# Two-layer hybrid block: attention stacks on the hardware DMA queue, out-projection operands prepared inside the attention, and four smaller moves

## The chip, the cores and the metric

One core of a Trainium2 chip runs the whole program. The metric is the device time of one execution in microseconds; the runs shown of a kernel are summed up by their median.

## The reference, cut to what matters

```python
def block(h_lat, h_ctx, l):                   # 1024 latent and 256 context tokens, D = 1024, two layers
    u = modulate(rms_norm(h), ...)            # modulation vectors from c and c_ctx
    p = u @ w_in                              # mLSTM | attention | pool | convolution, 256 wide each
    q, k = rope(rms_norm(q)), rope(rms_norm(k))          # 4 heads, 2 maps of width 32 each
    a = softmax(q0 @ k0.T) - lam * softmax(q1 @ k1.T)    # two maps per head
    y = concat(mlstm, subln(a @ v), pool, conv)
    h = h + gate1 * (y @ w_out)
    g, up = split(modulate(rms_norm(h), ...) @ ffn_w_in)
    h = h + gate2 * ((silu(g) * up) @ ffn_w_out)         # D_FF = 2816
...
```

In the second layer the context tokens are keys and values only; their queries, output projection and FFN are left out.

## The kernel before, in words

Every float32 matmul is three passes: operands are split into a high part (an ACT copy to float32r) and a low part (a subtraction on DVE or POOL, `sub_lo`, L292), and hi·hi, lo·hi and hi·lo are summed in PSUM. One helper, L165, records nearly all engine operations, so rows are told apart by tile names.

Each layer runs through five phases. **A** (`mixers`, L593): the projections of the normed input `uh`/`ul`, with the mLSTM, the convolution and the pool woven in; the weights come through `load_w` (two raw buffers, five of each part). `qk_in` (L945) norms and rotates queries and keys, splits them, and writes both parts to a DRAM scratch `qk_scr` (tile `qks`, L971 and L972) by DMAs issued on POOL, which use the software queue (q0). **B** (`attention`, L1152): `stacks(h)` reads for each of a head's two maps a stack of queries `Qs` (high part twice, then low part twice, 64 + 64 partitions, L1169 and L1170) and one of keys `Ks` (high and low part twice, 128 partitions, L1172), also on POOL, and the values `V` on SP (the hardware queue, q1). The doubling is in the source's access pattern: `dup` puts a leading dimension of size 2 and step 0 before the rows.

```python
            return AP(tensor=ap.tensor, offset=ap.offset, ap=[[0, 2]] + [list(x) for x in ap.ap])
```

The work is cut into units of a head and 256 queries, five per head in layer 0, four in layer 1. Each unit takes four slots of a hand-written plan, in which scores `sc`, softmax `pr`, transposes `aT`, values `po` and the head norm `subln` of several units overlap. The plan fixes the order on PE, ACT and DVE. `stacks(0)` is issued in slot 0, `stacks(1)` in slot 2, each later head's in slot 2 of the head before the one ahead of it; there are buffers for two heads. A score needs map 0 first and map 1 in the next slot.

**C** (`out_proj`, L1345): chunks of tokens, in layer 0 (256, 512), (768, 512), (0, 256) as (start, size), in layer 1 the first two. It loads `y` and splits it, loads the residual `h`, and for each of eight output tiles loads two weights (`wr`, two buffers), splits them (`wh` on ACT, `wl` on POOL) and multiplies. `norm_ffn` (L1395) norms the previous chunk beside the matmuls of the next, and makes the Strassen operands `Uh`/`Ul` of the FFN. **F** (`ffn_in`, L1464): 22 halves of products in Strassen form; in layer 0 the second layer's modulation (`mod_vec`, L441, two DVE passes over each `mw`) is advanced by 18 steps at the end of each half until it is done. **G** (`ffn_out`, L1580): the down-projection with `gr`, `xr` loaded and split as `gh`/`gl`, `xh`/`xl`; its pools open when `ffn_in`'s close.

Of the kernel before, what the change touches and what calls it, by code (L numbers as in the profile page):

```python
# [18 lines left out]
P = 128  # L19
# [165 lines left out]
class Builder:  # L185
# [32 lines left out]
    def stage(self, temps):  # L218

        if self.fx is not None:  # L220
            self.fx.close()
        self.fx = ExitStack()
        self.fp = self.mkpool(self.fx, "right")
        self.temps = (self.fp, 512, temps)
# [368 lines left out]
    def mixers(self, l, u, norm):  # L593
# [130 lines left out]
        return self.attention()  # L724
# [427 lines left out]
    def attention(self):  # L1152
# [3 lines left out]
        gd = nc.gpsimd.dma_start  # L1156
# [7 lines left out]
        def stacks(h):  # L1164
            Qs, Ks = [], []
            for m in range(2):
                mp = 2 * h + m
                Qm = self.U(f"Qs{m}", F32R)
                gd(Qm[0:64, q0:NT], dup(self.qk_scr[0, mp, 0, :, q0:NT]))  # L1169
                gd(Qm[64:P, q0:NT], dup(self.qk_scr[0, mp, 1, :, q0:NT]))  # L1170
                Km = self.U(f"Ks{m}", F32R)
                self.stack = gd(Km[:, 0:NT], dup(self.qk_scr[1, mp].rearrange("a r n -> (a r) n")))  # L1172
                Qs.append(Qm)
                Ks.append(Km)
            V = self.U("V")[:, :NCH * 64].rearrange("p (c x) -> p c x", x=64)
            nc.sync.dma_start(V, self.v_scr[h])
            heads[h] = (Qs, Ks, V)
# [166 lines left out]

    def out_proj(self, l, src, dst, chunks, later):  # L1345
# [3 lines left out]
        order = (0, 1, 4, 5, 6, 7, 2, 3)  # L1349
        todo = iter(())  # L1350
        first = ExitStack()
        ypool = self.mkpool(first, "left")
        for i, (c0, n) in enumerate(chunks):
            v = 1 if c0 < NCTX else 0
            cs = slice(c0, c0 + n)
            y = [None] * KT
            for k in order:
                if i == 0:
                    hi, lo = (ypool.tile([P, 512], F32R, name=f"{nm}{k}", tag=nm, bufs=KT) for nm in ("y0h", "y0l"))
                else:  # L1360
                    hi, lo = self.E("yh", KT, F32R), self.E("yl", KT, F32R)
                raw = self.E("yr", 3)
                hi, lo, raw = hi[:, :n], lo[:, :n], raw[:, :n]
                nc.sync.dma_start(raw, self.y_scr[k][:, cs])
                self.copy(hi, raw)
                self.sub_lo(lo, raw, hi)
                y[k] = (hi, lo)
            h = [self.E("h", 10) for _ in range(KT)]
            for k in range(KT):
                nc.sync.dma_start(h[k][:, :n], src(k)[:, cs])  # L1370
            for nt in range(KT):
                w = []
                for pc in range(2):
                    raw, hi, lo = self.E("wr", 2), self.E("wh", 3, F32R), self.E("wl", 3, F32R)
                    nc.sync.dma_start(raw, self.a["w_out"][l, nt, pc])
                    self.copy(hi, raw)
                    self.sub_lo(lo, raw, hi, nc.gpsimd)
                    w.append((hi, lo))
# [10 lines left out]
            if i == 0:  # L1389
                first.close()  # L1390
# [5 lines left out]
    def norm_ffn(self, l, need):  # L1396
# [9 lines left out]
        def chunk(h, c0, n):  # L1406
# [11 lines left out]
            cs = slice((c0 - NCTX) // 2, (c0 - NCTX) // 2 + HALF)  # L1418
            a, b = slice(0, HALF), slice(HALF, 2 * HALF)
            for k in range(4):  # L1420
                for x in (k, k + 4):
                    nc.vector.scalar_tensor_tensor(h[x], h[x], A[:, x, v:v + 1], r, ALU.mult, ALU.mult)
                    nc.scalar.activation(h[x], h[x], AF.Identity, bias=B(x))
                yield
                u1, u2 = h[k], h[k + 4]
                t, z = self.T("t12"), self.T("t34")
                g = nc.gpsimd.tensor_tensor
                g(t[:, a], u1[:, b], u1[:, a], ALU.subtract)
                nc.vector.tensor_tensor(z[:, a], u2[:, b], u1[:, b], ALU.subtract)
                g(t[:, b], u2[:, b], t[:, a], ALU.subtract)  # L1430
                g(z[:, b], u2[:, a], t[:, b], ALU.subtract)
                yield
                Uh, Ul = state["U"][k]
                two = lambda x: x.rearrange("p (i n) -> p i n", i=2)
                for i, j, src in ((0, 1, u1[:, a].unsqueeze(1)), (1, 3, two(u2)), (3, 5, two(t)), (5, 7, two(z))):
                    hi, lo = Uh[:, i:j, cs], Ul[:, i:j, cs]
# [27 lines left out]
    def ffn_in(self, l, state, mid, need, side):  # L1464
# [6 lines left out]
        more = 0 if need else 3  # L1471

        def weights(f, x):
            raw = {}
            for i, (ff, pc) in enumerate(((f, 0), (f, 1), (f + 1, 0), (f + 1, 1))):
                raw[i] = self.E("fr", 8 + more)
                nc.sync.dma_start(raw[i], self.a["ffn_in"][l, ff, x, pc])
            for i in (self.S1, self.S2, self.S3, self.S4):
                raw[i] = self.E("fr", 8 + more)
# [7 lines left out]
        def split(raw):  # L1487
            hi, lo = self.E("fh", 5 + more, F32R), self.E("fl", 5 + more, F32R)
# [65 lines left out]
        for f in range(0, NF, 2):  # L1554
            sg = sc = None
            for x in range(2):
# [11 lines left out]
                for _ in range(18):  # L1568
                    next(side, None)
            for i, (ff, ab) in enumerate(((f + 1, 1), (f + 1, 0), (f, 1), (f, 0))):  # L1570
                dst = self.g_scr[ff][:, 0:1024].rearrange("p (c h n) -> p c h n", c=2, h=2)[:, :, ab, :]
                nc.sync.dma_start(dst, sg[i].rearrange("p (c n) -> p c n", c=2))
# [7 lines left out]
    def ffn_out(self, l, src, dst, chunks, later):  # L1580

        nc = self.nc
        todo = iter(())
        for c0, n in chunks:
# [6 lines left out]
            for f in range(NF):  # L1591
                gr, gh, gl = self.E("gr", 3)[:, :n], self.E("gh", 3, F32R)[:, :n], self.E("gl", 3, F32R)[:, :n]
                nc.sync.dma_start(gr, self.g_scr[f][:, at:at + n])
                wr, wh, wl = self.E("xr", 2, n=D), self.E("xh", 2, F32R, D), self.E("xl", 2, F32R, D)
                nc.sync.dma_start(wr, self.a["ffn_out"][l, f])
                self.copy(gh, gr)
                self.sub_lo(gl, gr, gh)
                for x in range(2):
                    s = slice(x * 512, x * 512 + 512)
                    self.copy(wh[:, s], wr[:, s])  # L1600
                    self.sub_lo(wl[:, s], wr[:, s], wh[:, s])
                for nt in range(KT):
                    s = slice(nt * P, nt * P + P)
# [12 lines left out]
            todo = itertools.chain(todo, later(h, c0, n))  # L1616
        for _ in todo:
            pass

    def run(self):  # L1620
        nc, a = self.nc, self.a
        self.fx = None
# [17 lines left out]
        for l in range(DEPTH):  # L1640
            need = l < DEPTH - 1
            ch = LATE if need else LATE[:2]
            self.tok = CHUNKS if l == 0 else LATE
# [3 lines left out]
            self.mixers(l, u, later)  # L1647
            self.mx.close()
            self.ux.close()
# [4 lines left out]
            self.out_proj(l, src, mid, ch, norm)  # L1654
            self.phase("F")
            self.stage(6)
# [3 lines left out]
            self.stage(5)  # L1660
# [13 lines left out]
            self.fx = None  # L1674
# [84 lines left out]
```

## Time and profile before

| what | us |
|---|---|
| median of 3 runs (3423.34 to 3432.39) | 3426.58 |
| the profiled execution, whole | 3416.67 |
| its span on the chip | 3414.10 |
| TensorE busy | 3001.4 (88 %) |
| VectorE, ScalarE, GpSimd busy | 1935.2, 1338.8, 913.3 |
| both attentions with their starts (560 to 800, 2340 to 2580) | 240 and 240, TensorE busy 173 and 168 |
| both out-projections (800 to 980, 2580 to 2741) | 180 and 161, TensorE busy 141 and 109 |

Read it as a string of stages. In the FFN and the projections TensorE is busy all the time and the other engines have room. In the attentions and the out-projections it is not: there the reader looks for the wait that ends last. A row of the timeline gives the start, the duration, engine, line, operation and tiles, the count, and in brackets the idle time before it with what ended it.

### The profile page before, as it was taken

The page shows a single profiled execution, that of the slowest core. Times are in us where ns is not written, and L with a number is a line of the kernel's source. Part 1 is how long each engine was busy: PE and PEld are TensorE (multiplying, and loading weights), DVE is VectorE, ACT ScalarE, POOL GpSimd, SP SyncE. Part 2 cuts the span into 40 slices and gives each one's busy share as a digit, 9 for nine tenths or more (in the row PEclk, how much of TensorE's full clock was granted, in tenths as well). Part 3 has the DMA queues.
Part 4 walks back from the last instruction along what each step waited for, and adds up shares of the span by engine and source line. Part 5 has one row for each costly group of instructions (what it writes and reads, how often), then busy time and mean ns, then how long its engine had stood idle before and what let it go on. Part 6 is the DMA issues. An engine that isn't in the chain of part 4 may idle for free. (4 is left out here: it accounts for less than half of the span.)

```text
span 3414.1 us, 43736 instructions
## 1 busy us (share of the span) xinstructions
PE 3001.4 (88%) x16144; PEld 2397.6 (70%) x16144; DVE 1935.2 (57%) x2975; ACT 1338.8 (39%) x2605; POOL 913.3 (27%) x698
## 2 busy tenths in 40 slices
PE   7999885786978999998999898975787699999999
PEld 3766664665656787887887787764565488888787
DVE  6494565883557887333334749564882655444333
ACT  4212443774442222232334622443883533332332
POOL 2240321322532323222000124231322444332000
PEclk9999987898988999999999999988898899999999
DMA  7123435224424443222654411235215232221653
GB/s 268 56 71 99 100 79 95 42 43 154 138 77 136 144 143 124 62 72 92 205 173 151 147 38 44 76 88 90 55 34 170 87 96 87 82 80 55 211 173 130
DMA packets 253877, 363.96 MB, mean 107 GB/s; under 512 B 76768, under 2 KB 125536, under 8 KB 253664
## 3 DMA queue, kind: packets, MB, share of 16 engines
q1 hardware_dynamic: 196896, 331.10, 30.7%
q0 software_dynamic: 56768, 30.07, 5.2%
q8 instruction: 127, 2.08, 0.3%
q14 instruction: 86, 0.70, 0.1%
HBM read 291.70 MB, written 69.21 MB: 106 GB/s over the span
## 5 line engine op out<-in xcount | busy, mean ns | idle before, releaser
L165 PE MATMUL fps<-Uh,fh 128*128 128x512 f32 (+1 forms) x1288 | 496.9, 386 | 38.3 <-ACT fh L165 33.3
L165 PE MATMUL fps<-Uh,fl 128*128 128x512 f32 (+1 forms) x1288 | 494.1, 384 | 1.0 <-DVE fl L165 1.0
L165 PE MATMUL fps<-Ul,fh 128*128 128x512 f32 (+1 forms) x1288 | 495.0, 385 | 0.0
L165 ACT ACTIVATE fh<-fr 128x512 fp32r<-128x512 f32 x330 | 206.9, 631 | 548.7 <-PE fps L165 416.8
L165 DVE TENSOR_TENSOR fl<-fr,fh 128x512 fp32r<-128x512 f32 x330 | 274.2, 835 | 158.6 <-ACT fh L165 158.0
L165 PE MATMUL xps<-gh,xh 128*128 128x512 f32 (+1 forms) x880 | 327.5, 374 | 23.5 <-ACT xh L165 23.5
L165 PE MATMUL xps<-gh,xl 128*128 128x512 f32 (+1 forms) x880 | 325.3, 373 | 5.3 <-DVE xl L165 5.2
L165 PE MATMUL xps<-gl,xh 128*128 128x512 f32 (+1 forms) x880 | 325.5, 372 | 0.0
L165 DVE TENSOR_TENSOR xl<-xr,xh 128x512 fp32r<-128x512 f32 x220 | 143.0, 688 | 305.1 <-ACT xh L165 304.9
L165 PEld LDWEIGHTS fps<-Uh,fh 128*128 128x128 f32 x1288 | 246.1, 191 | 92.6 <-ACT fh L165 34.9
L165 DVE TENSOR_TENSOR ft<-fps,ft 128x512 f32<-128x512 f32 (+1 forms) x230 | 152.9, 665 | 237.6 <-PE fps L165 237.4
L165 PEld LDWEIGHTS fps<-Uh,fl 128*128 128x128 f32 x1288 | 245.5, 191 | 51.6 <-issue 2.9
L165 PEld LDWEIGHTS fps<-Ul,fh 128*128 128x128 f32 x1288 | 246.4, 191 | 44.0 <-issue 0.8
L165 ACT ACTIVATE xh<-xr 128x512 fp32r<-128x512 f32 x220 | 127.0, 623 | 324.9 <-PE xps L165 309.1
L165 DVE TENSOR_REDUCE ls<-sc 128x1 f32<-128x1280 f32 (+1 forms) x144 | 195.1, 1367 | 83.8 <-PE sc L165 83.2
L165 PE MATMUL sc<-Ks,Qs 128*128 128x512 f32 (+1 forms) x400 | 127.7, 429 | 124.8 <-ACT pr L165 66.4
L165 PE MATMUL fmps<-uh,wfh 128*128 128x512 f32 (+1 forms) x592 | 222.9, 376 | 14.0 <-ACT kT L165 14.0
L165 PE MATMUL fmps<-ul,wfh 128*128 128x512 f32 (+1 forms) x592 | 222.9, 377 | 0.0
L165 PE MATMUL fmps<-uh,wfl 128*128 128x512 f32 (+1 forms) x592 | 221.2, 374 | 0.0
L165 ACT ACTIVATE pr<-sc,ls 128x1280 f32<-128x1280 f32 (+1 forms) x144 | 178.4, 1239 | 91.3 <-DVE ls L165 90.3
L165 PEld LDWEIGHTS xps<-gh,xh 128*128 128x128 f32 x880 | 168.2, 192 | 54.6 <-ACT xh L165 25.9
L165 DVE SCALAR_TENSOR_TENSOR acc<-cy,par,acc 128x1286 f32<-128x1286 f32 (+28 forms) x120 | 194.2, 1656 | 1.0
(311 smaller groups left out, 6317.6 us busy)
## 6 DMA issues: line engine op xcount, KB each, us to landing
xr<-in_ffn_out SPq DMA_DIRECT2D x110, 512.0 KB, 3.5
fr<-in_ffn_in SPq DMA_DIRECT2D x176, 256.0 KB, 2.8
mw<-in_mod_w SPq DMA_DIRECT2D x160, 256.0 KB, 3.1
gs<-ft SPq DMA_DIRECT2D x99, 256.0 KB, 2.2
gr<-gs SPq DMA_DIRECT2D x88, 256.0 KB, 3.6
wr<-in_w_out SPq DMA_DIRECT2D x80, 256.0 KB, 2.9
wfr<-in_w_fm SPq DMA_DIRECT2D x56, 256.0 KB, 2.7
Ks<-qks POOLq DMA_DIRECT2D x16, 640.0 KB, 23.6
```

The costliest lines, as they stand in the source:

```text
L165: ins = f(*args, **kw)
```

## The change

The Q and K stacks and the writes to `qk_scr` are issued on SP instead of POOL, with the same access patterns. The pool of `load_w` moves to its own stack and lives through the out-projection, whose weights now go through `load_w`. `out_early` runs one step in each slot of the attention from the second unit of the last head (ten steps: six tiles of `y` and four weights of the first chunk). In layer 1 the out-projection's second chunk of 512 is cut into two of 256, and the Strassen halves are blocks of 128 tokens. `mod_vec` takes 10 steps per half. In `ffn_out` the weights come in halves of 512 with five buffers, `gr` is gone, and the tiles of the first `f` come from a pool that is open during `ffn_in`.

```diff
+        self.wx = ExitStack()
+        self.wp = self.mkpool(self.wx, "right")
-        self.wp = self.mkpool(self.mx, "left")
...
-        nc.gpsimd.dma_start(self.qk_scr[kind, 4 * i:4 * i + 4, 0, :, c0:c0 + n], hi)
-        nc.gpsimd.dma_start(self.qk_scr[kind, 4 * i:4 * i + 4, 1, :, c0:c0 + n], lo)
+        for x, v in enumerate((hi, lo)):
+            nc.sync.dma_start(self.qk_scr[kind, 4 * i:4 * i + 4, x, :, c0:c0 + n].bitcast(F32), v.bitcast(F32))
...
-        gd = nc.gpsimd.dma_start
+        gd = nc.sync.dma_start
...
-                gd(Qm[0:64, q0:NT], dup(self.qk_scr[0, mp, 0, :, q0:NT]))
-                gd(Qm[64:P, q0:NT], dup(self.qk_scr[0, mp, 1, :, q0:NT]))
+                for x in range(2):
+                    gd(Qm[x * 64:x * 64 + 64, q0:NT].bitcast(F32), dup(self.qk_scr[0, mp, x, :, q0:NT].bitcast(F32)))
                 Km = self.U(f"Ks{m}", F32R)
-                self.stack = gd(Km[:, 0:NT], dup(self.qk_scr[1, mp].rearrange("a r n -> (a r) n")))
+                self.stack = gd(Km[:, 0:NT].bitcast(F32),
+                                dup(self.qk_scr[1, mp].rearrange("a r n -> (a r) n").bitcast(F32)))
...
+        last_head = 4 * 3 * len(nblk) + 4
...
+            if k >= last_head:
+                next(early, None)
...
+    def load_y(self, hi, lo, k, cs):
+
+        self.nc.sync.dma_start(lo.bitcast(F32), self.y_scr[k][:, cs])
+        self.copy(hi, lo.bitcast(F32))
+        self.sub_lo(lo, lo.bitcast(F32), hi)
...
+    def out_w(self, l, nt, pc):
+        return self.load_w(self.a["w_out"][l, nt, pc], 512, self.nc.gpsimd, "wo")
+
+    def out_early(self, l, chunk):
+
+        self.y0, self.w0 = {}, []
+        for i, k in enumerate(self.YORDER[:6]):
+            self.first_y(k, *chunk)
+            yield
+            if i < 4:
+                self.w0.append(self.out_w(l, i // 2, i % 2))
+                yield
...
-                w = []
-                for pc in range(2):
-                    raw, hi, lo = self.E("wr", 2), self.E("wh", 3, F32R), self.E("wl", 3, F32R)
-                    nc.sync.dma_start(raw, self.a["w_out"][l, nt, pc])
-                    self.copy(hi, raw)
-                    self.sub_lo(lo, raw, hi, nc.gpsimd)
-                    w.append((hi, lo))
+                w = [self.w0.pop(0) if self.w0 else self.out_w(l, nt, pc) for pc in range(2)]
...
-                for _ in range(18):
+                for _ in range(10):
                     next(side, None)
...
-                gr, gh, gl = self.E("gr", 3)[:, :n], self.E("gh", 3, F32R)[:, :n], self.E("gl", 3, F32R)[:, :n]
-                nc.sync.dma_start(gr, self.g_scr[f][:, at:at + n])
-                wr, wh, wl = self.E("xr", 2, n=D), self.E("xh", 2, F32R, D), self.E("xl", 2, F32R, D)
-                nc.sync.dma_start(wr, self.a["ffn_out"][l, f])
+                early = f == 0 and not done
+                if early:
+                    gh, gl = self.T("gh", F32R)[:, :n], self.T("gl", F32R)[:, :n]
+                else:
+                    gh, gl = self.E("gh", 3, F32R)[:, :n], self.E("gl", 3, F32R)[:, :n]
+                nc.sync.dma_start(gl.bitcast(F32), self.g_scr[f][:, at:at + n])
...
+                    if early and x == 0:
+                        wr, wh, wl = (self.T(nm, d) for nm, d in zip(("xr", "xh", "xl"), dt))
+                    else:
+                        wr, wh, wl = (self.E(nm, 5, d) for nm, d in zip(("xr", "xh", "xl"), dt))
...
+            oc = LATE if need else ((256, 512), (768, 256), (1024, 256))
...
-            self.out_proj(l, src, mid, ch, norm)
+            self.out_proj(l, src, mid, oc, norm)
+            self.phase("F")
+            self.fx.close()
+            self.tx.close()
+            self.wx.close()
```

Start of layer 0's attention: on POOL before, the stacks of the first head (4658 to 4666) and the second's first query stack, without the row numbers.

```order
L1169 DMA Qs_4658<-qks_430 64x1x1280 [waits DMASW0_49,PE_49]
L1170 DMA Qs_4658<-qks_430 64x1x1280 [waits DMASW1_49]
L1172 DMA Ks_4661<-qks_430 128x1x1280 [waits PE_49]
L1169 DMA Qs_4663<-qks_430 64x1x1280 [waits PE_49]
L1170 DMA Qs_4663<-qks_430 64x1x1280 [waits DMASW4_49]
L1172 DMA Ks_4666<-qks_430 128x1x1280 [waits DMASW5_49,PE_49]
L1169 DMA Qs_4695<-qks_430 64x1x1280 [waits DMASW6_49,PE_49]
```

The same place on SP in the changed kernel (`vs` is the scratch of the values, `so`/`os` and `ys` are the mLSTM's output on its way to `y`).

```order
L690 DMA vs_431<-avt 128x4x64 [waits DMAHW1_49,Activation_49]
L1176 DMA Qs_4658<-qks_430 64x1x1280 [waits DMAHW2_49,PE_49]
L1176 DMA Qs_4658<-qks_430 64x1x1280 [waits DMAHW3_49]
L941 DMA so<-os_433 128x256 [waits DMAHW7_49,DMAHW4_49,DVE_49]
L690 DMA vs_431<-avt 128x4x64 [waits DMAHW5_49,Activation_49]
L1178 DMA Ks_4661<-qks_430 128x1x1280 [waits DMAHW6_49,PE_49]
L1176 DMA Qs_4663<-qks_430 64x1x1280 [waits PE_49]
L948 DMA ys_432<-so 128x2x128 [waits DMAHW0_49,Activation_49]
L1176 DMA Qs_4663<-qks_430 64x1x1280 [waits DMAHW1_49]
L1178 DMA Ks_4666<-qks_430 128x1x1280 [waits DMAHW2_49,PE_49]
L1183 DMA V<-vs_431 128x640 [waits DMAHW5_49,DMAHW3_49,PE_49]
L1176 DMA Qs_4695<-qks_430 64x1x1280 [waits DMAHW4_49,PE_49]
```

The same transfers stand in the same order, now on one engine with the stores and the values; `V` stands behind the first head's stacks.

On PE, the last rows of layer 0's attention (`ams`) and the first of the out-projection, before.

```order
L165 MATMUL ams<-cst,ar 64x128 x3
L165 MATMUL ops<-y0h_6640,wh 128x512 [waits Activation_49]
L165 MATMUL ops<-y0l_6641,wh 128x512 [waits DVE_49]
L165 MATMUL ops<-y0h_6640,wl 128x512 [waits Pool_49]
L165 MATMUL ops<-y0h_6646,wh 128x512
```

The same place in the changed kernel, to the last tile of `y`.

```order
L165 MATMUL ams<-cst,ar 64x128 x3
L165 MATMUL ops<-y_6112,woh 128x512 x2
L165 MATMUL ops<-y_6112,wol 128x512
L165 MATMUL ops<-y_6161,woh 128x512 x2
...
L165 MATMUL ops<-y_6686,woh 128x512 x2
L165 MATMUL ops<-y_6686,wol 128x512
L165 MATMUL ops<-y_6690,woh 128x512 [waits Activation_49]
L165 MATMUL ops<-y_6690,woh 128x512 [waits DVE_49]
```

The first matmul waits for nothing that the attention hasn't waited for; the first wait stands at the eighth tile of `y`.

On SP, the weights of layer 1's first projection (`wtr<-in_w_vg`) before: they stand between the last stores of `ffn_in` (`gs`), ahead of `ffn_out`'s loads.

```order
L299 DMA wtr<-in_w_vg 128x544 [waits DMAHW0_49,PE_49]
L299 DMA wtr<-in_w_vg 128x544 [waits DMAHW1_49]
L1572 DMA gs_8003<-ft 128x2x256 [waits DMAHW2_49,Pool_49]
L1574 DMA gs_8003<-ft 128x2x256 [waits DMAHW3_49,DVE_49]
L299 DMA wtr<-in_w_vg 128x544 [waits DMAHW4_49,DMAHW0_49,Pool_49]
```

And in the changed kernel, where they stand behind the last stores of `ffn_out` (`hscr`).

```order
L1657 DMA hscr<-h 128x256 [waits DMAHW7_49,DVE_49]
L1657 DMA hscr<-h 128x256 [waits DMAHW0_49,DVE_49]
L304 DMA wtr<-in_w_vg 128x544 [waits DVE_49,DMAHW1_49,PE_49,Pool_49]
L304 DMA wtr<-in_w_vg 128x544 [waits DMAHW2_49]
```

They moved behind all of `ffn_out`, since the pool now lies where `ffn_out`'s tiles lie.

## Rows read from the trace of the kernel before

**Rows 1.** Timeline of PE, first scores of each layer's attention: start, us, engine, operation, [idle before].

```profile
578.41 1.41 PE L165 MATMUL sc<-Ks,Qs 128*128 128x512 f32 x3 [25.91 <-DMA Ks<-qks]
2384.94 2.40 PE L165 MATMUL sc<-Ks,Qs 128*128 128x512 f32 x5 [29.97 <-DMA Ks<-qks]
```

**Rows 2.** Timeline of POOL, the first issue of the stacks in layer 0.

```profile
545.90 0.70 POOL L1169 DMA_DIRECT2D Qs<-qks  x1 [8.74 <-PE tmps L165]
```

**Rows 3.** Windows while a later head's stacks land; the last two columns: DMA share, GB/s.

```profile
640.00:642.00 2.00, 0.84 (x4) 0.49 (x3) 1.10 (x1) 2.00 (x4) 2.00 (x1) 1.00 0.90 184
650.00:652.00 2.00, 1.65 (x11) 1.32 (x11) 1.89 (x3) 1.92 (x5) 0.83 (x1) 1.00 0.29 105
652.00:654.00 2.00, 1.29 (x7) 0.96 (x7) 1.44 (x2) 2.00 (x4) 2.00 (x1) 1.00 0.24 57
2496.00:2498.00 2.00, 2.00 (x27) 1.70 (x25) 1.93 (x5) 0.88 (x2) 0.00 (x0) 1.00 0.20 53
```

**Rows 4.** DMA: SP's queue from 545 to 655 (packets, MB); issues: count, KB each, median us to landing.

```profile
q1 hardware_dynamic: 1845, 1.94, 9.4%
...
Ks<-qks POOLq DMA_DIRECT2D x16, 640.0 KB, 23.6
...
Qs<-qks POOLq DMA_DIRECT2D x16, 320.0 KB, 19.8
...
Qs<-qks POOLq DMA_DIRECT2D x16, 256.0 KB, 18.4
```

**Rows 5.** The same score of two neighbouring units (PE's timeline), then five units' window.

```profile
2432.58 0.84 PE L165 MATMUL sc<-Ks,Qs 128*128 128x512 f32 x3 [0.99 <-ACT pr L165]
...
2442.51 0.84 PE L165 MATMUL sc<-Ks,Qs 128*128 128x512 f32 x3 [0.99 <-ACT pr L165]
...
2425.00:2475.00 50.00, 41.47 (x365) 31.47 (x364) 44.27 (x53) 43.78 (x83) 21.85 (x16) 1.00 0.30 63
```

**Rows 6.** Timeline of PE, first matmul of each out-projection, and a steady one in layer 1.

```profile
816.44 0.80 PE L165 MATMUL ops<-y0h,wh 128*128 128x512 f32 x1 [19.80 <-ACT wh L165]
...
2595.09 0.79 PE L165 MATMUL ops<-y0h,wh 128*128 128x512 f32 x1 [18.59 <-ACT wh L165]
2595.68 0.63 PE L165 MATMUL ops<-y0l,wh 128*128 128x512 f32 x1
```

**Rows 7.** Timeline, layer 0's last chunk (256): one weight's load and split; first and last output.

```profile
971.33 2.01 SPq L1375 DMA_DIRECT2D wr<-in_w_out  x2
...
974.13 0.63 ACT L165 ACTIVATE wh<-wr 128x512 fp32r<-128x512 f32 x1 [2.07 <-DMA wr<-in_w_out]
...
974.84 1.27 POOL L292 TENSOR_TENSOR wl<-wr,wh 128x512 fp32r<-128x512 f32 x1 [1.86 <-ACT wh L165]
...
935.30 0.48 DVE L165 SCALAR_TENSOR_TENSOR h<-ops,mod,h 128x256 f32<-128x256 f32 x1 [2.98 <-PE ops L165]
...
980.06 0.48 DVE L165 SCALAR_TENSOR_TENSOR h<-ops,mod,h 128x256 f32<-128x256 f32 x1 [3.15 <-PE ops L165]
```

**Rows 8.** Layer 1: window of the second chunk (PE, PEld, DVE, ACT, POOL busy); then PE's timeline.

```profile
2648.00:2703.00 55.00, 47.97 (x193) 33.54 (x195) 34.37 (x39) 26.95 (x47) 29.70 (x25) 0.94 0.38 115
...
2702.56 0.39 PE L165 MATMUL ops<-yh,wl 128*128 128x512 f32 x1
...
2733.77 0.58 PE L165 MATMUL fps<-Uh,fh 128*128 128x256 f32 x1 [24.71 <-ACT fh L165]
```

**Rows 9.** Window of layer 0's FFN input with the modulation beside it.

```profile
1030.00:1180.00 150.00, 134.70 (x676) 109.33 (x676) 123.50 (x169) 37.79 (x63) 44.82 (x29) 0.94 0.44 140
```

**Rows 10.** Timeline of PE, first matmul of each FFN output.

```profile
1615.80 0.80 PE L165 MATMUL xps<-gh,xh 128*128 128x512 f32 x1 [9.39 <-ACT xh L165]
...
3168.92 0.80 PE L165 MATMUL xps<-gh,xh 128*128 128x512 f32 x1 [7.50 <-ACT xh L165]
```

**Rows 11.** Timeline of PE, first projection of layer 1.

```profile
1953.99 0.47 PE L165 MATMUL tmps<-wth,uh 128*128 128x272 f32 x1
...
1965.45 0.57 PE L165 MATMUL tmps<-wth,uh 128*128 128x272 f32 x1 [5.09 <-DVE Z L165]
```

More of the change, by code (lines that the diff above doesn't have):

```diff
@@ L216, in E, with stage @@
         return self.fp.tile([P, n], dt, tag=tag, name=tag, bufs=bufs)
-    def stage(self, temps):
+    def stage(self, temps=None):
         if self.fx is not None:
             self.fx.close()
+        if temps:
+            if self.tx is not None:
+                self.tx.close()
+            self.tx = ExitStack()
+            self.temps = (self.mkpool(self.tx, "right"), 512, temps)
         self.fx = ExitStack()
         self.fp = self.mkpool(self.fx, "right")
-        self.temps = (self.fp, 512, temps)
     def S(self, name, dt=F32):
@@ L590, in tm_gen, with mixers @@
             yield c
-    def mixers(self, l, u, norm):
+    def mixers(self, l, u, norm, early_out):
         nc, a = self.nc, self.a
@@ L723, in mixers @@
         self.phase("B")
-        return self.attention()
+        return self.attention(early_out)
     def mix(self, a, n, b):
@@ L1150, in conv, with attention @@
                 yield
-    def attention(self):
+    def attention(self, early):
         nc, l = self.nc, self.l
@@ L1342, in attention, with first_y @@
         return ya
+    YORDER = (0, 1, 4, 5, 6, 7, 2, 3)
+    def load_y(self, hi, lo, k, cs):
+        self.nc.sync.dma_start(lo.bitcast(F32), self.y_scr[k][:, cs])
+        self.copy(hi, lo.bitcast(F32))
+        self.sub_lo(lo, lo.bitcast(F32), hi)
+    def first_y(self, k, c0, n):
+        t = self.U(f"y{k}", F32R)
+        hi, lo = t[:, 0:n], t[:, 512:512 + n]
+        self.load_y(hi, lo, k, slice(c0, c0 + n))
+        self.y0[k] = (hi, lo)
+    def out_w(self, l, nt, pc):
[8 more added lines that the diff above has]
+                yield
     def out_proj(self, l, src, dst, chunks, later):
         nc = self.nc
-        order = (0, 1, 4, 5, 6, 7, 2, 3)
+        order = self.YORDER
         todo = iter(())
-        first = ExitStack()
-        ypool = self.mkpool(first, "left")
         for i, (c0, n) in enumerate(chunks):
@@ L1355, in out_proj @@
             cs = slice(c0, c0 + n)
[L1356 to L1364, printed above, removed]
-                self.copy(hi, raw)
-                self.sub_lo(lo, raw, hi)
-                y[k] = (hi, lo)
-            h = [self.E("h", 10) for _ in range(KT)]
+            if i == 0:
+                for k in order[6:]:
+                    self.first_y(k, c0, n)
+                y = self.y0
+            else:
+                y = {}
+                for k in order:
+                    y[k] = self.E("yh", KT, F32R)[:, :n], self.E("yl", KT, F32R)[:, :n]
+                    self.load_y(*y[k], k, cs)
+            h = [self.E("h", 9) for _ in range(KT)]
             for k in range(KT):
@@ L1389, in out_proj @@
             if i == 0:
-                first.close()
+                self.ux.close()
             todo = itertools.chain(todo, later(h, c0, n))
@@ L1424, in chunk @@
                 yield
-                u1, u2 = h[k], h[k + 4]
+                half = lambda x, i: x[:, :n].rearrange("p (s i j) -> p s i j", i=2, j=P)[:, :, i, :]
+                (u1a, u2a), (u1b, u2b) = ((half(h[k], i), half(h[k + 4], i)) for i in range(2))
                 t, z = self.T("t12"), self.T("t34")
                 g = nc.gpsimd.tensor_tensor
-                g(t[:, a], u1[:, b], u1[:, a], ALU.subtract)
-                nc.vector.tensor_tensor(z[:, a], u2[:, b], u1[:, b], ALU.subtract)
@@ L1435, in chunk @@
-                for i, j, src in ((0, 1, u1[:, a].unsqueeze(1)), (1, 3, two(u2)), (3, 5, two(t)), (5, 7, two(z))):
-                    hi, lo = Uh[:, i:j, cs], Ul[:, i:j, cs]
+                two = lambda x: x[:, :n].rearrange("p (i s j) -> p i s j", i=2, j=P)
+                for i, j, src in ((0, 1, u1a.unsqueeze(1)),
+                                  (1, 3, h[k + 4][:, :n].rearrange("p (s i j) -> p i s j", i=2, j=P)),
+                                  (3, 5, two(t)), (5, 7, two(z))):
+                    hi, lo = (x[:, i:j, cs].rearrange("p i (s j) -> p i s j", j=P) for x in (Uh, Ul))
@@ L1470, in ffn_in @@
         gp, vc = nc.gpsimd.tensor_tensor, nc.vector.tensor_tensor
-        more = 0 if need else 3
+        more = 0 if need else 1
         def weights(f, x):
@@ L1475, in weights @@
             for i, (ff, pc) in enumerate(((f, 0), (f, 1), (f + 1, 0), (f + 1, 1))):
-                raw[i] = self.E("fr", 8 + more)
+                raw[i] = self.E("fr", 8 + 3 * more)
                 nc.sync.dma_start(raw[i], self.a["ffn_in"][l, ff, x, pc])
             for i in (self.S1, self.S2, self.S3, self.S4):
-                raw[i] = self.E("fr", 8 + more)
+                raw[i] = self.E("fr", 8 + 3 * more)
             A11, A12, A21, A22, S1, S2, S3, S4 = range(8)
@@ L1582, in ffn_out @@
         nc = self.nc
-        todo = iter(())
+        todo, done = iter(()), False
         for c0, n in chunks:
@@ L1616, in ffn_out @@
             todo = itertools.chain(todo, later(h, c0, n))
+            done = True
         for _ in todo:
@@ L1659, in run @@
             self.phase("G")
-            self.stage(5)
+            self.stage()
             if need:
```

53 lines of the change are left out of this document (32 added, 21 removed).

## The prediction, made before the changed kernel was run

> **What bounds the kernel now.** I read four views: the windows by stage, which tell where TensorE has room; its timeline there, for the waits; the DMA issues and windows, for what the waits hang on; then the order of the change. In the FFN and the projections TensorE is busy all the time and the change leaves its passes alone. So what is to be had lies at the seams.
>
> The two largest waits are the attentions' starts: TensorE idles 25.91 and 29.97 us for a Ks transfer [rows 1]. The first stack is issued at 545.90, when the projection frees its buffer [rows 2]; the first score runs at 578.41. These transfers are slow: 23.6 us to landing for 640 KB, 18 to 20 for a Qs [rows 4]. Once the attention runs, it takes 9.93 us per unit (2432.58 to 2442.51), with DVE busy 44.3 of 50 us and ACT 43.8 [rows 5]; later stacks land beside it unseen.
>
> Why they are slow is the point on which I decide. While a head's six transfers are in flight, 0.90 of the DMA engines are busy at 184 GB/s. Towards the end the rate drops in steps, to 105 with a share of 0.29, then to 57 with 0.24; another head's end shows 53 with 0.20 [rows 3]. A transfer with all engines at its disposal would take them until it is done. Here most engines stand idle while the last Ks still crawl: one transfer has some two or three engines' worth, two have twice that. Six side by side fill most of the 16; one alone moves some 53 GB/s. So a stack transfer, as its access pattern stands, is narrow, and what made the head's load bearable was that the six went over different engines. The change keeps the pattern, with its leading dimension of 2, and changes the queue.
>
> **The change, part by part.** The sum is made against the profiled execution (3416.67 us, of which 3414.10 span), 9.9 below the median of the runs shown; 9.9 is added back at the end. Gains are positive.
>
> *Stacks on SP.* A head needs 4 x 320 + 2 x 640 KB = 2.62 MB in layer 0 and 4 x 256 + 2 x 640 KB = 2.36 MB in layer 1 [rows 4]. No row shows a narrow transfer on the hardware queue, so I bound it. Upper end: all six over many engines; half a head's bytes at 184 GB/s are 7 us, with 2 for landing the first score comes at about 555 in place of 578.4, and 21 us earlier in layer 1: together +44. Lower end: all on the same few engines, one after the other at 53 GB/s: 49.5 and 44.5 us per head. SP's own transfers (1.94 MB in 110 us, two heads' time [rows 4]) have a sixteenth of their bytes on each engine: some 2 us a head at half of 53 GB/s per engine, if two share it. So 51.5 and 46.5. A head's units take 5 x 9.93 = 49.7 and 4 x 9.93 = 39.7 us: the attention then runs at the pace of its loads. Layer 0: the fourth head is complete at 545.9 + 4 x 51.5 + 2 = 753.9; its units take 49.7, and behind the last slot come 19.4 more (796.6 - 578.4 - 4 x 49.7, where 796.6 is 816.44 less its idle 19.80 [rows 6]). End 823.0, 26 later than now. Layer 1, with loads from about 2353, 2 us ahead of the idle time of rows 1 (an estimate): complete at 2541, plus 39.7, plus 32.8 by the same reckoning (2576.5 - 2384.9 - 4 x 39.7): 2613.5 against 2576.5, 37 later. Together -63. [...] The buffers for two heads do not help, since each next stack finds its buffer free just as the engines come free.
>
> [...]
>
> *Out-projection prepared early.* Removes the idle 19.80 and 18.59 us before the first matmul, and the slow first ones behind it (0.63 us in layer 1's second, 0.39 in a steady row [rows 6, 8]; some 14 of them at about 0.2 are 3 us per layer): 44. Left is the last tile of `y`, for which PE now waits at its eighth tile: 3 per layer. The ten steps each cost ACT 0.63 us, as for a weight [rows 7], and DVE or POOL a subtraction, in slots where both are nearly nine tenths busy [rows 5]: 0 to 7 per layer, I take 5. 44 - 6 - 10 = +28, between 15 and 38.
>
> *Layer 1 in 256s.* A weight is now used for half the columns. Per output tile two weights must go through load, ACT and POOL; the last chunk of layer 0, which is 256 wide, gives one output per (980.06 - 935.30) / 7 = 6.4 us, where one weight goes from SP at 971.33 to POOL's end at 976.1 [rows 7] with two raw buffers, as in the change. So 8 x 6.4 = 51, then 45 for the third chunk with half the norm beside it: 96, for 55 now [rows 8]: -41. The tail (2703 to 2733.8, 31 us [rows 8]) ends on half the tokens and takes about 18: +13. Together -28, between -40 and 0, as the deeper buffers for the split parts may help.
>
> *Modulation spread.* Where it runs, DVE is busy 123.5 of 150 us and TensorE idles 15.3 [rows 9]. At 10 steps per half, some nine per half being needed over all 22, it fits beside the products: +10, between 0 and 15.
>
> *First operands of the FFN output.* The gaps of 9.39 and 7.50 us [rows 10] shrink to about 3 each, since the second weight half still waits for the old pools: +11, between 5 and 15.
>
> *Layer 1's first weights.* They stood ahead of `ffn_out` and now stand behind its last stores; a load, ACT and POOL pass lie before the first projection. It had started at 1953.99, and idled 5.09 us for other things at 1965.45 [rows 11], which hides part: -10, between -16 and -3.
>
> The rest (`qk_scr` writes on SP, five buffers of halves) I cost at nothing: TensorE has other work there. If SP stands waiting for POOL's low part with a weight load behind it, that may be 5 us a layer.
>
> Sum: -63 + 28 - 28 + 10 + 11 - 10 = -52. Profiled 3469; with 9.9, **3478 us**.
>
> **The rivals.** *The stacks go over different engines also from SP* (faster). For it: on POOL they do, at 184 GB/s for six. Against it: nothing but the queue would choose the engines. The stacks then give +34 (same first-head rate, but no issue costs) to +44 in place of -63: with the others' +11 that is 3372 to 3382, and 3350 if the 256s cost little. It decides from about 65 GB/s for one head's transfers on: at 70 a head takes 37 and 34 us, under its units' time, and the starts are 4 us worse than now each. *The stacks are slow, but the small parts are all at their good ends* (about no change): the 256s at -10, the early operands at 38, the modulation at 15 give -63 - 10 + 38 + 15 + 11 - 10 = -19, and with the early operands of the FFN output at 15 and the weights at -3 about -8: 3435. For it: all these lie within rows; against: all at once. *The stores behind the stacks are held up too* (slower still): SP issues the values and the mLSTM stores between them, and each has a share of the narrow engines; each head of both layers could start 4 us later, 8 x 4 on top: 3510.
>
> **How the numbers follow.** 0.3 % of the time, some 10 us, is what a measurement can tell from no change. Rows 3 show the narrowness and the unchanged pattern; only the choice of engines is open. I give the serial case 0.66, of it 0.05 to the third rival, and 0.06 more to no change; the spread case 0.28. The forecast's own range is 3442 to 3510. Two in ten may be left out: 0.05 above, some 0.13 below, which cuts into the spread case: 3364 to 3512. Faster 0.28, same 0.06, slower 0.66.
>
> **What would show it.** Right: Ks lands 12 us or more after issue with DMA share near 0.15 all through the attention; a score at the head of each new head waits for a DMA; first scores still near 573. Wrong: first scores near 555 and no such waits. The early operands show in `ops` directly behind the last `ams`; the 256s in a wait for POOL before each output of layer 1's last two chunks; the spread modulation in a DVE share below 0.8 from 1030 on; the weights in a gap of some 10 us before the first `tmps` of layer 1.

## The result, and the profile after

The changed kernel takes 3510.8 us (median of 4 runs, 3509.24 to 3513.39) against 3424.96: ratio 1.025, interval 1.0229 to 1.0271, slower by 86 us. The forecast was 3478, slower, in a range of 3364 to 3512: the time lies 33 us above the forecast and 1 us inside the range.

The page of the changed kernel, parts 1, 3 and 4: busy time, the one data queue that is left, and the chain that ended last by engine and line. TensorE is busy 37 us longer, the chain spends 4 % of the span on Ks transfers.

```profile
PE 3038.5 (87%) x16354; PEld 2432.8 (69%) x16354; DVE 1950.9 (56%) x3022; ACT 1356.1 (39%) x2664; POOL 875.4 (25%) x634
...
q1 hardware_dynamic: 251024, 365.19, 33.0%
...
PE fps L165 12%; PE xps L165 6%; DMA Ks<-qks 4%; PE ops L165 2%; PE po L165 1%; DVE h L165 1%; ACT pr L165 0%; DVE ls L165 0%; PE sc L165 0%; SPq L1176 0%; POOL wol L297 0%; PE tmps L165 0%; PE atp L165 0%; DVE Ul L165 0%; DMA wor<-in_w_out 0%
```

PE's timeline of the changed kernel at the scores that waited for a stack (start, us, operation, [idle before]); these answer to [rows 1]. Layer 0 is above, layer 1 below; in each, the first two rows are maps 0 and 1 of the first head, the others the first score of a later head.

```profile
584.86 1.40 PE L165 MATMUL sc<-Ks,Qs 128*128 128x512 f32 x3 [11.78 <-DMA Ks<-qks]
611.12 2.26 PE L165 MATMUL sc<-Ks,Qs 128*128 128x512 f32 x5 [24.86 <-DMA Ks<-qks]
715.23 1.41 PE L165 MATMUL sc<-Ks,Qs 128*128 128x512 f32 x3 [3.81 <-DMA Ks<-qks]
768.51 0.81 PE L165 MATMUL sc<-Ks,Qs 128*128 128x512 f32 x3 [3.61 <-DMA Ks<-qks]
...
2422.79 1.41 PE L165 MATMUL sc<-Ks,Qs 128*128 128x512 f32 x3 [25.26 <-DMA Ks<-qks]
2446.11 1.83 PE L165 MATMUL sc<-Ks,Qs 128*128 128x512 f32 x4 [21.91 <-DMA Ks<-qks]
2492.55 1.19 PE L165 MATMUL sc<-Ks,Qs 128*128 128x512 f32 x2 [5.29 <-DMA Ks<-qks]
2540.61 1.41 PE L165 MATMUL sc<-Ks,Qs 128*128 128x512 f32 x3 [6.71 <-DMA Ks<-qks]
2588.88 1.41 PE L165 MATMUL sc<-Ks,Qs 128*128 128x512 f32 x3 [5.37 <-DMA Ks<-qks]
```

The last two heads of layer 0 start 53.3 us apart (715.23 to 768.51) and those of layer 1 48.2: the pace of the loads, for which the prediction had 51.5 and 46.5. Layer 0's second head waited for no stack. Map 1 comes 26 and 23 us behind map 0. Three windows of the changed kernel inside that time (PE, PEld, DVE, ACT, POOL busy, granted clock, DMA share, GB/s) answer to [rows 3]:

```profile
586.00:590.00 4.00, 0.27 (x2) 0.00 (x0) 3.63 (x5) 1.69 (x3) 0.00 (x0) 0.50 0.13 52
...
598.00:602.00 4.00, 0.00 (x0) 0.00 (x0) 0.00 (x0) 0.00 (x0) 0.00 (x0) 0.50 0.13 52
660.00:670.00 10.00, 7.79 (x72) 5.88 (x70) 7.73 (x10) 8.03 (x18) 1.50 (x1) 1.00 0.13 53
```

With up to six stack transfers queued, 0.13 of the engines are busy, two of 16, at 52 to 53 GB/s: what one Ks alone made on the software queue [rows 3], now for all of them together. SP's own timeline has long issues in that time, which I read as the queue backing up into the issuing engine: an issue takes 0.6 us where stacks are wide (below) and up to 15.8 here.

```profile
602.53 5.61 SPq L1178 DMA_DIRECT2D Ks<-qks  x1
608.22 12.15 SPq L1176 DMA_DIRECT2D Qs<-qks  x2
620.46 13.02 SPq L1178 DMA_DIRECT2D Ks<-qks  x1
633.58 12.14 SPq L1183 DMA_DIRECT2D V<-vs  x1
```

Two readings fit these windows: all stacks share one pair of engines, or the queue works off one transfer at a time, each on a pair of its own. The packets of a wide load tell them apart. The load `so` (128 rows of 1 KB) is issued at 555.67, behind two query stacks. The DMA view of the changed kernel from 556 to 558, 558 to 570 and 570 to 572:

```profile
DMA packets 137, 0.17 MB, mean 86 GB/s; under 512 B 14, under 2 KB 126, under 8 KB 137
...
DMA packets 573, 0.67 MB, mean 56 GB/s; under 512 B 464, under 2 KB 464, under 8 KB 573
...
DMA packets 99, 0.10 MB, mean 50 GB/s; under 512 B 70, under 2 KB 86, under 8 KB 99
```

The packets between 512 B and 2 KB are the rows of `so`: 112 at once, none for 12 us, then 16. That is the share of fourteen engines of 16 ahead of the stacks, and the share of two behind them. So here the stacks are on one pair, and the 16 rows of `so` that lie on that pair waited with them.

Stage by stage, from PE's timelines (last work before the first score; first score; start of the last head norm's row; first FFN product; first FFN output; first `fmps`, the wide projection of layer 1; and so on), in us of duration:

| stage | before | after | e1 | e5 | combined |
|---|---|---|---|---|---|
| to the end of layer 0's projections | 552.5 | 573.1 | 563.4 | 537.0 | 533.0 |
| wait for the first score | 25.9 | 11.8 | 2.2 | 3.3 | 3.2 |
| attention, layer 0 | 216.7 | 264.1 | 234.1 | 232.0 | 226.0 |
| its end to the FFN | 189.5 | 167.3 | 163.9 | 165.6 | 164.2 |
| FFN input, layer 0 | 631.2 | 607.4 | 607.9 | 607.7 | 609.0 |
| FFN output and start of layer 1 | 376.0 | 390.2 | 389.9 | 391.1 | 389.9 |
| rest of layer 1's projections | 363.2 | 383.6 | 386.0 | 348.8 | 348.9 |
| wait for the first score | 29.9 | 25.3 | 7.8 | 6.8 | 7.8 |
| attention, layer 1 | 190.5 | 245.2 | 208.7 | 208.9 | 196.3 |
| its end to the FFN | 158.4 | 167.4 | 167.9 | 168.0 | 136.3 |
| FFN input, layer 1 | 435.1 | 426.4 | 427.7 | 427.6 | 426.9 |
| FFN output to TensorE's last work | 241.0 | 245.8 | 245.4 | 245.7 | 248.1 |

### The profile page after: what moved, and what is told of

Read it like the earlier page. It is cut to its first block, busy times and chain, and to the rows that moved or that the text cites. A ratio compares the mean times of both kernels' runs of the same rounds, so it can differ in the third digit from the quotient of the medians.

```text
span 3511.6 us, 44759 instructions
## 1 busy us (share of the span) xinstructions
PE 3038.5 (87%) x16354; PEld 2432.8 (69%) x16354; DVE 1950.9 (56%) x3022; ACT 1356.1 (39%) x2664; POOL 875.4 (25%) x634
## 5 line engine op out<-in xcount | busy, mean ns | idle before, releaser
L165 PEld LDWEIGHTS fps<-Uh,fl 128*128 128x128 f32 x1288 | 245.2, 190 | 50.3 <-DVE fl L165 1.7
L165 PEld LDWEIGHTS sc<-Ks,Qs 128*128 128x128 f32 x400 | 76.1, 218 | 220.4 <-issue 107.0
L165 DVE TENSOR_TENSOR gl<-gl,gh 128x512 fp32r<-128x512 f32 (+1 forms) x110 | 70.9, 644 | 264.4 <-ACT gh L165 264.1
L1223 POOL TENSOR_TENSOR pr<-pr,pr 128x1280 f32<-128x1280 f32 (+1 forms) x36 | 95.9, 2663 | 422.7 <-DVE pr L165 225.0
```

The costliest lines, as they stand in the source:

```text
L165: ins = f(*args, **kw)
L1223: nc.gpsimd.tensor_tensor(pr[0][:, :n], pr[0][:, :n], pr[1][:, :n], ALU.add)
```

## The experiments

**e1: wide stacks on SP.** The doubling moves behind the rows, in the order of both stacks alike; the four products of high and low parts stay.

```diff
-                for x in range(2):
-                    gd(Qm[x * 64:x * 64 + 64, q0:NT].bitcast(F32), dup(self.qk_scr[0, mp, x, :, q0:NT].bitcast(F32)))
-                self.stack = gd(Km[:, 0:NT].bitcast(F32),
-                                dup(self.qk_scr[1, mp].rearrange("a r n -> (a r) n").bitcast(F32)))
+                for x in range(2):
+                    gd(Qm[x * 64:x * 64 + 64, q0:NT].bitcast(F32),
+                       AP(tensor=qa.tensor, offset=qa.offset, ap=[[NT, 32], [0, 2], [1, NT - q0]]))
+                    self.stack = gd(Km[x * 64:x * 64 + 64, 0:NT].bitcast(F32),
+                                    AP(tensor=ka.tensor, offset=ka.offset, ap=[[NT, 32], [32 * NT, 2], [1, NT]]))
```

> The changed kernel, with the sources of the stacks put so that a row dimension of 32 leads and the doubling stands second (four transfers per map in place of three, same bytes, still on SP, writes of the scratch as in the change). Theory N (a stack transfer is cut by its leading dimension of 2 and all of them run on the same two DMA engines, at 52 to 54 GB/s, so a head takes some 50 us): a head's stacks land within 10 to 15 us, first scores come 8 to 12 us after the first issue in both layers, no score of a later head waits for a DMA, the attentions end 60 us earlier each, and the time is 3375 to 3400 us. Rival Q (the order on SP's queue holds them up: waits, stores and values between the stacks, whatever the width): heads still start late, 3470 us or more.

Measured: 3410.49 us, 100 less than the change; ratio to before 0.9947 (0.9924 to 0.9969). First scores come 2.2 and 7.8 us after the projections, and no later head waits. The windows of this kernel while the first two heads' stacks land, and one SP issue, show what the same bytes do on all engines:

```profile
566.00:568.00 2.00, 0.36 (x3) 0.04 (x1) 1.97 (x3) 0.00 (x0) 0.00 (x0) 0.63 0.96 243
568.00:570.00 2.00, 0.00 (x0) 0.00 (x0) 1.96 (x4) 1.62 (x3) 0.00 (x0) 0.50 1.01 220
570.00:575.00 5.00, 1.86 (x5) 1.60 (x6) 1.03 (x3) 3.36 (x6) 0.00 (x0) 0.50 1.04 241
```

```profile
566.47 0.59 SPq L1181 DMA_DIRECT2D Ks<-qks  x1
```

So N holds and Q falls: SP's order is the same. But the time is 10 us above the expected range: the attentions are still 17 and 18 us longer than before.

**e2: stacks back on POOL** (`gd = nc.gpsimd.dma_start`, and the `bitcast`s of the stacks go).

> The changed kernel with the stacks alone back on POOL's queue, narrow as they are; the scratch is still written from SP. Theory N: the six transfers of a head go over different engines again, first scores come 26 to 32 us after the last projection as before, later heads wait for nothing; the attentions lose 45 us each against the change: 3405 to 3430 us. Rival Q gives the same here. What is left of the first layers' projections (in the change 10 us longer in layer 0, 24 us in layer 1) must stay if the writes on SP cause it.

Measured 3448.78 us, 62 less than the change, 19 above the upper end expected, and above before (ratio 1.006, 1.0036 to 1.0083). First scores wait 25.2 and 27.7 us, and no later head waits, as N said; but the attentions are 231 and 208 us, 33 and 37 less than in the change in place of 45. So the narrow stacks on SP explain 62 of the 86 us by this comparison, and something that has nothing to do with the stacks' queue costs the attentions 14 and 18 us.

**e3: writes of the scratch back on POOL**, stacks as in the change.

> The changed kernel with the writes of the scratch alone back on POOL; the stacks stay on SP. If the writes on SP (four leading rows, and an issue that waits for POOL's low part with loads behind it) cost the projections their 34 us, the first scores come that much earlier: 3470 to 3485 us. If that loss has another cause (the last loads of the mLSTM's output behind the query stacks, layer 1's late first weights), little moves: 3500 to 3512 us.

Measured 3484.79 us: 26 less than the change, at the upper end expected. Layer 1's projections are at 366.0 us again, layer 0's at 566.8. What stays of layer 0's, some 14 us, is mostly the mLSTM's output: in both kernels its last load is issued behind two query stacks and DVE waits for it (12.54 us in e3; the row is of the changed kernel).

```profile
571.85 0.43 DVE L165 TENSOR_TENSOR hs<-hs,so 128x256 f32<-128x256 f32 x1 [12.11 <-DMA so<-os]
```

**e4: the kernel before, its stacks on SP.** The queue alone.

> The kernel before with one thing changed: the stacks are issued on SP, with the same narrow patterns. Theory N: first score some 14 us earlier than 26 to 32 us after the projections in map 0, map 1 some 25 us behind it, a stall of 3 to 7 us at each later head, attentions 40 to 55 us longer each: 3500 to 3530 us. Without the pair of engines fixed (stacks over several pairs): 3385 to 3410 us.

Measured 3485.63 us, ratio 1.0167 (1.0138 to 1.0197), 58 above before: less than expected here, and close to the 63 us of the prediction's term. Attentions 245 and 229 us, so 28 and 38 longer. In its trace layer 0's projections end 17.9 us later, since DVE waits 12.22 us for the same load of the mLSTM's output, and that layer's attention ends 32 us later. Layer 1's ends 33 us later, counted from the end of the projections. The prediction had 26 and 37.

**e5: wide writes.** e1, with the scratch laid out so that a write's destination leads with 128 rows.

```diff
-        self.qk_scr = self.dp.tile([2, 8, 2, 32, NT], F32R, name=f"qks{l}")
+        self.qk_scr = self.dp.tile([2, 2, 8, 32, NT], F32R, name=f"qks{l}")
...
+            nc.sync.dma_start(self.qk_scr[kind, x, 4 * i:4 * i + 4].rearrange("m r n -> (m r) n")[:, c0:c0 + n].bitcast(F32), v.bitcast(F32))
```

> The first experiment's kernel (wide stacks on SP) with the scratch laid out so that a write has 128 leading rows and can use all 16 DMA engines; the writes stay on SP, at the same places of its order. If the projections lost their time because a write of four leading rows is slow (theory W), layer 1's projection stage comes back from 386 to about 366 us and layer 0's by 6: 3380 to 3390 us. If they lost it because SP stands waiting for the values to be written while the next rope tables and weights stand behind (theory H), the width changes nothing: 3405 to 3412 us.

Measured 3350.33 us, 60 below e1, and 30 below what W expected: W holds, H falls, and there is more. The projections are now 15 us shorter than in the kernel before, in both layers. The scratch's transfers point to the reason; this is the view of tile `qks` in layer 1's projections, of before and of e5, its last line:

```profile
DMA to landing us min/median/max: 4.7/8.4/10.4
```

```profile
DMA to landing us min/median/max: 1.7/2.0/3.7
```

A write frees the buffer that it reads 6 us sooner, and ACT's waits for the two written tiles (15.3 us in layer 1 of the kernel before) are gone. That the 15 us come from there is argued, not shown: the writes have also left POOL, and no run issues wide writes from POOL. In the change the transfers behind a narrow write waited as well. The view of the waits, layer 1's projections, changed kernel, then e5, shows the rope tables and the mLSTM's output:

```profile
POOL gq L970 <- DMA ropec<-in_rope: 32.1, 5, 9.9
...
DVE hs L165 <- DMA so<-os: 18.5, 4, 5.1
```

```profile
POOL gq L970 <- DMA ropec<-in_rope: 19.8, 4, 6.0
```

In e1, which differs from e5 in the layout of the scratch alone, the two waits are 31.1 and 19.5 us; in e5 the second is 0.3.

**e6: e1 with the writes on POOL.**

> The first experiment's kernel with the writes of the scratch back on POOL's queue, narrow as before. Theories W and H both expect 3380 to 3390 us, with the first projections as long as in the kernel before (layer 1's stage about 364 us). With the run before it decides: W if both come down, H if this one alone does.

Measured 3384.55 us, as both expected; with e5 it decides for the width. 26 us below e1, the same 26 as e3 below the change.

**e7: the ten steps in the attention's tail** (`last_head = 4 * 4 * len(nblk)`, and what is left of the steps runs behind the last slot; on e6).

> The kernel of the run before it (wide stacks on SP, writes on POOL), with the ten steps that prepare the out-projection begun after the last unit's last slot, in place of the second unit of the last head. Theory S (each step puts a copy on ACT and a subtraction on DVE or POOL into the chain of a full slot, some 1.7 us a step, which is why the attentions stay 17 us longer even with wide stacks): both attentions come back to 217 to 222 and 190 to 196 us from first score to last head norm, the out-projections still start within 4 us, and the time is 25 to 35 us less than the run before. If the lengthening comes from the stacks' landing on SP instead, under 8 us less.

Measured 3362.78 us, 22 below e6: short of S's 25 to 35, and far above the 8 of the other case. Attentions 225.9 and 195.0 us, layer 0's above the 222 expected. Why a step costs so much shows in e1's last head, DVE's timeline, then ACT's:

```profile
2500.48 1.48 DVE L165 TENSOR_REDUCE ls<-sc 128x1 f32<-128x1280 f32 x1
2504.03 0.69 DVE L165 TENSOR_TENSOR y<-y 128x512 fp32r<-128x512 f32 x1 [2.07 <-ACT y L165]
2504.64 1.49 DVE L165 TENSOR_REDUCE ls<-sc 128x1 f32<-128x1280 f32 x1
```

```profile
2502.06 1.33 ACT L165 ACTIVATE pr<-sc,ls 128x1280 f32<-128x1280 f32 x1 [0.89 <-DVE ls L165]
2503.28 0.19 ACT L165 ACTIVATION_READ_ACCUMULATOR pr<-sc,ls 128x1 f32 x1
2503.38 0.62 ACT L165 ACTIVATE y<-y 128x512 fp32r<-128x512 f32 x1
```

In the fixed order the subtraction stands ahead of DVE's next maximum, and it needs a copy that stands behind ACT's exponential of this slot. For this tile DVE idles 2.07 us and then works 0.69. Over the six tiles the idle time before a subtraction and the subtraction come to 18.0 us in layer 0 and 18.8 in layer 1, near the 17.4 and 18.2 by which e1's attentions are longer.

**e8: layer 1's chunk of 512 whole** (`oc = ch`; on e6).

> The kernel of e6 with layer 1's out-projection in two chunks of 512 again, in place of 512 and two of 256; the rest of the change stays. Theory C (a weight goes through load, ACT and POOL twice as often per column): that out-projection, 166 us from its first matmul to the FFN's in the change, comes back to 136 to 142, and the time falls by 22 to 30 us against e6. If the weights had waited for something else, by less than 8.

Measured 3358.88 us, 26 below e6, as C expected; the stage is 135.6 us from its first matmul in place of 167.4.

**e9: combined** (e5, e7 and e8 in one kernel).

> The change with four corrections: stacks and scratch writes on SP with wide patterns (e5), the ten steps in the attention's tail (e7), layer 1's second chunk of 512 whole (e8). If the three effects lie in different stages and add up: 3350 - 22 - 26 = about 3303 us (3295 to 3312), projections 537 and 349 us long, attentions 226 and 195, layer 1's out-projection 136. If they overlap, 3315 or more.

Measured 3298.75 us (3296.0 to 3305.62, 4 runs), ratio to before 0.9624 (0.961 to 0.9638): the effects add. It beats both kernels, the changed one by 212 us. No first score waits longer than this:

```profile
536.23 1.07 PE L165 MATMUL sc<-Ks,Qs 128*128 128x512 f32 x3 [3.25 <-DMA Ks<-qks]
...
2281.97 1.41 PE L165 MATMUL sc<-Ks,Qs 128*128 128x512 f32 x3 [7.79 <-DMA Ks<-qks]
```

**e10: operands late** (`last_head = 10 ** 6`, so that the steps stand behind the last slot; on e9).

> The combined kernel with the ten steps placed behind the attention's last slot, so that nothing of the out-projection is prepared ahead. Theory S: the attentions get back the 9 and 5 us that they still lose to the steps in their tail (217 and 190 us), and the out-projections start 15 to 20 us later again with slow first matmuls: 18 to 28 us slower than the combined kernel.

Measured 3301.79 us, ratio 0.9633 (0.9617 to 0.965): within what the two can be told apart, so the expectation fell. The attentions are 219.3 and 192.6 us, and the out-projection starts directly behind them all the same:

```profile
753.61 1.10 PE L165 MATMUL ams<-cst,ar 128*64 128x128 f32 x8
754.63 0.80 PE L165 MATMUL ops<-y,woh 128*128 128x512 f32 x1
```

What closes the gap of [rows 6] is not the place of the steps in the slots. In this kernel two or three `y` loads at a time go out behind the attention's last stores, and the first weights wait ready, since their buffers are free during the attention. In the kernel before, all of them were issued behind the last store. But what the attentions got back the out-projections lost: from their first matmul to the FFN they take 172.1 and 141.7 us, for 163.1 and 135.3 in the combined kernel.

**e11: 18 steps of the modulation** (on e9).

> The combined kernel with 18 steps of the modulation per half in place of 10. The FFN input of layer 0, 608 us in the changed kernels against 631 before, holds two edits: the spread and the early operands of the FFN output (7 to 8 us as of now). If the spread is worth the rest: 12 to 18 us slower than the combined kernel; if the early operands are all of it, under 4.

Measured 3320.51 us, 22 above e9; the FFN input of layer 0 takes 624.9 us for 609.0. The spread is worth 16 us there; the other 6 are scattered over several stages, and I have no cause for them.

**e12: half of the bytes narrow** (on e9, queries with `dup`, keys in wide pieces).

> The combined kernel with the query stacks narrow again (the doubling leads, two engines) and the key stacks wide (in pieces of 32 rows): half of a head's bytes in layer 0, 1.31 MB, and 1.05 MB in layer 1 go over the pair. Theory N gives 25 and 20 us for them at 53 GB/s, under a head's units (50 and 40 us): first scores come 12 to 16 us after the first issue in place of 3, the second map another 12 behind, no later head waits for a DMA, and the time is 25 to 45 us above the combined kernel's. If any narrow transfer on SP costs what the change's did, wherever the rate stands, later heads wait too: 60 us or more above.

Measured 3336.63 us, 38 above e9, inside the range of N. Some 14 of them lie ahead of the attention, in layer 0's projections, where DVE waits 13.16 us for the last load of the mLSTM's output. First scores wait for both maps, later heads for none; the granted clock is at 0.50 in the window below. PE's timeline at layer 0's start, then a window between its two rows:

```profile
552.00 1.41 PE L165 MATMUL sc<-Ks,Qs 128*128 128x512 f32 x3 [4.67 <-DMA Ks<-qks]
569.88 2.47 PE L165 MATMUL sc<-Ks,Qs 128*128 128x512 f32 x6 [16.48 <-DMA Ks<-qks]
```

```profile
561.00:565.00 4.00, 0.00 (x0) 0.00 (x0) 0.00 (x0) 0.00 (x0) 0.00 (x0) 0.50 0.13 52
```

## Why the prediction was right, and where it was wrong

**The deciding step held.** "All on the same few engines, one after the other at 53 GB/s" is what the windows show: 0.13 and 52 to 53 GB/s, with up to six transfers queued. The term was -63; e4, which makes this one move, gives -58. That one head's stacks set the pace from a certain rate on held too: at half the bytes no later head waits (e12). That SP would begin every stack on the same engines, no row of the kernel before shows: to take -63, the lower of its two bounds, was the author's estimate. What the runs show is two engines of 16, by the shares, and one pair for all, by the packets of `so`. One sign was missed: first scores were to come "still near 573" and came at 584.86, with map 1 at 611.12, as the projections ended 20.6 us later.

**"The rest ... I cost at nothing" failed.** The writes of the scratch on SP cost 26 us (e3, and again e1 against e6); the bound given was 5 per layer. The prediction looked at SP's waiting for POOL's low part; e5, with the same order and wide writes, shows that the wait was not it. The pattern that made the stacks narrow was noted for them and not for the writes, whose destination leads with 4.

**The third rival had a mechanism right and its size wrong.** It said that what SP issues between the stacks has a share of the narrow engines and is held up, 4 us a head. The packets of `so` show that share, 16 of 128 rows. But what cost time was this one load ahead of layer 0's attention, some 10 us (573.1 to 563.4 us, change against e1), and not every head. Its 3510 agrees with the measured time by luck.

**The steps of the early operands were mis-sized.** "0 to 7 per layer, I take 5": measured 17.4 and 18.2 (e1's attentions against before), most of which e7 and e10 give back. The price was counted as engine time in nearly full slots; what it cost was a wait between two pinned orders, about 2 us before each subtraction. The gain was about right: 44 less 6 predicted, 22 us in layer 0 (189.5 to 167.3) and, without the 256s, 22 in layer 1 (158.4 to 136.3 in the combined kernel). So the part brought some 9 us, not 28. And by e10 the kernel is as fast without any step in the slots.

**The 256s held:** -28 predicted, 26 measured (e8), by the price per output tile of [rows 7]: in the change the two chunks take 100 us and the tail 20, for 96 and 18 predicted. **The modulation** brought 16 in its stage, 22 in all (e11), more than its upper bound of 15. The window of [rows 9], from which the bound came, does not hold all of it: in the kernel before TensorE waits for the modulation (`macc`) again at 1338.99, 5.78 us.

**The first FFN operands and layer 1's first weights held.** These are the changed kernel's rows, on PE: the second weight half in each FFN output, and the first projection of layer 1.

```profile
1630.05 0.80 PE L165 MATMUL xps<-gh,xh 128*128 128x512 f32 x1 [3.48 <-ACT xh L165]
...
3268.47 0.79 PE L165 MATMUL xps<-gh,xh 128*128 128x512 f32 x1 [3.84 <-ACT xh L165]
...
1979.63 0.59 PE L165 MATMUL tmps<-wth,uh 128*128 128x272 f32 x1 [12.16 <-ACT wth L165]
```

The gaps of 9.39 and 7.50 us are gone from the FFN input, and 3.48 and 3.84 come back in the FFN output, "about 3 each" as said: 9.6 gained for a predicted 11. The gap before the first `tmps` is there, and from the last FFN output to the first `fmps` it takes 50.0 us for 41.0: 9 lost for a predicted 10. The other 5 of that stage's 14 us (376.0 to 390.2) and the 5 of the last FFN output lie in the FFN outputs themselves; beyond the 3.48 and 3.84, one to two us in each have no cause shown.

With the measured sizes (the FFN inputs, 24 and 9, and the two FFN output stages, -14 and -5, by the table): -58 - 26 + 9 - 26 + 24 + 9 - 14 - 5 = -87. The medians differ by 86 us, the profiled spans by 97.5 (3414.1 to 3511.6), since the profiled execution of the kernel before lies 8 us under its median and that of the change 3 above. The sum mixes differences of medians with stages of single executions, so part of its closeness is luck. Against the -52 of the prediction, the writes cost 26 more and the early operands brought 19 less, while the stacks and the modulation came out 5 and 6 better. The direction and its cause were foreseen; that the time fell 1 us inside the range is luck.

## What to carry to other kernels

Before a transfer moves to the hardware queue, look at what its access pattern leads with. Here, with a doubling in front, all stacks together moved at 52 to 53 GB/s on 0.13 of the engines, and of a wide load issued behind two of them 16 of 128 rows came 12 us late. Putting the rows first took one transfer more per map and was worth 100 us here; writes that lead with 128 rows in place of four were worth another 60. And a step put into a pinned order is priced by what it makes the next engine wait for (2.07 us ahead of one subtraction here), not by its own time (0.69).

## What the runs showed of the hardware

The same stacks moved at 52 to 53 GB/s from SP with the doubling in front, and at 220 to 243 with 32 rows in front (e1). The median SP issue took 0.33 us in the kernel before and 0.37 in the change. But in the change 43 of 1452 issues took over 2 us, up to 15.8, all of them between 559 and 763 and between 2398 and 2575, where the narrow stacks are issued. In the kernel before, with the stacks on POOL, one of 1210 did (2.31). In e1, which has wide stacks on the same queue, the issues from 550 to 580, with the first heads' stacks among them, took 0.33 to 0.65.

Of the wide load `so`, issued behind two narrow stacks in the change, 112 of 128 rows moved at once and 16 some 12 us later. With four leading rows in the writes from SP, rope loads held POOL for 32.1 us in layer 1 of the change (31.1 in e1), and with 128 for 19.8 (e5). In layer 1 a wide write from SP landed in 2.0 us (median, e5) where POOL's narrow one took 8.4 in the kernel before; how late SP's narrow ones landed the traces do not tell.
